# A hybrid decoder block on one core: softmax rows divided at the head's output, a scaling in eight steps, head products two tiles behind, and one Strassen product split in the led pairs

## The chip, the cores and the metric

The kernel runs as one program on 1 core of one Trainium2 chip. The metric is the time of one execution on the device in microseconds (us), the median of several runs. TensorE (PE) makes the matrix products and the transposes, VectorE (DVE), ScalarE (ACT) and GpSimd (POOL) the work on vectors, and SyncE (SP) issues the transfers, in the order of its queue.

## The reference

```python
hn = rmsnorm(h, norm_mix)
(fq, fk, fv, ff, gq, gk, gv, ga, gb, gz, gate_fox, gate_gdn) = split_in(hn @ w_in)
# forgetting attention, 8 heads of 128, causal, 1024 positions
s = fq @ fk.T * Dh ** -0.5 + (c[:, None] - c[None, :])      # c: cumulative log of the forget gate
y_fox = softmax(where(causal, s, -inf)) @ fv
# gated delta rule on conv + silu of gq, gk, gv, in chunks of 64
u = inverse(I + A) @ (beta * (v - decayed k @ state)); o = q @ state + attn @ u
y_gdn = rmsnorm(o, gdn_norm) * silu(gz)
y = sigmoid(gate_fox) * (y_fox @ w_branch_fox) + sigmoid(gate_gdn) * (y_gdn @ w_branch_gdn)
h = h + y @ w_out
up = causal_dwconv(rmsnorm(h, norm_ffn) @ w_up, ffn_conv_w)  # 3 taps, 2 x 2816 channels
u_gate, u_val = split(up, 2)
out = rmsnorm(h + (silu(u_gate) * u_val) @ w_down, norm_final)
```

Sequence and model width are 1024, one layer, one sequence, all in float32. (These lines are a condensed form of the reference; the delta rule is written as one step of its chunked form.)

## The kernel before

Every large product is made in float32 precision from two fp32r parts, high (`h`) and low (`l`), by three matmuls: high by high, low by high, high by low. `split` makes them: ACT casts the high part (L106), DVE or POOL subtracts it to get the low part (L107).

The stages follow one another: `head_in` (normalises x, transposes it, starts the small projections; 0 to 121 us), `project` (32 Strassen jobs of 84 matmuls, 121 to 821 us), the mix of attention and delta rule (to about 1094 us), the merge of the branches (to 1261), `mix_out` (to about 1390), `ffn_up` (to 1799) and `ffn_down`. The large products go through `strassen`, Winograd's form with seven half-size products a job of 12 matmuls each (P1 to P7 by the block that they take: `11`, `21`, `t2`, `t3`, `t1`, `22`, `t4`). The bank `a` gathers P1, then t2, t1 and 22 on top, and ACT copies it out between them as `x1`, `x2`, `x3` (L258), so the next product into `a` waits for the copy; DVE adds `c` (L289, L300, L315) from banks and copies. The first jobs of a stage can be *led*: `lead` holds products already made ahead, so that job has no P1 of its own between `t1` and `22`. This is so for the first pairs of `ffn_up`.

In `project` other work runs between the matmuls, paced by `left`, the matmuls still to do (from 2688 down): the convolutions of the heads, then `inverse`, a forward substitution of all 64x64 triangular blocks at once on DVE (`invz`, `invt`; L949 the scaling by beta, `invb`, then L961 and L963 a product and a subtraction for each of its pieces). `inverse` yields after each piece; `project` takes `INVERSE_STEPS` of them evenly between the start and the point where 480 matmuls are left.

In the mix, PE alternates between two streams. `fox` takes head after head: `probs` makes the scores of eight tiles t of 128 queries (softmax row by row: DVE adds the bias and finds the maximum, L1113, ACT makes the exponential and its sum, L1119, DVE the reciprocal, L1120, and the row is scaled, on ACT at L1122 for t under 5 or in head 0, else on POOL in two halves, L1125); `attend` transposes the rows (L1146), splits them, and makes the product with the values in halves of four tiles into the bank `ya` (L1137); ACT copies it out as `ye` (L1165), and SP writes it. The `scan` is the delta rule: per chunk the products into one of three banks `us` (L1260, L1265, L1271, L1272, L1274), with `su` (ACT, L1267), `sr` and `ss` (DVE), the output `o` (DVE, L1282) and its square sum `sjk` (ACT, L1284). `prep` loads a head's inputs for the scan (`skt`, `svt` and others) and POOL scales two of them (L1234).

The order on PE is that of the program. The order on DVE, ACT, POOL and SP is chosen when the kernel is built, by a scheduler with a cost model, except where `keep_in_program_order` holds an instruction to its place. Each queue runs strictly in order.

Of the kernel before, what the change touches and what calls it, by code (L numbers as in the profile page):

```python
# [17 lines left out]
P = 128  # L18
# [3 lines left out]
NT = S // P  # L22
# [53 lines left out]
def inverse_pieces(m):  # L76

    n = m + 1
    step = 512 // n
    return [(c0, min(c0 + step, Q)) for c0 in range(n, Q, step)]  # L80


INVERSE_STEPS = 10 + sum(len(inverse_pieces(m)) for m in range(Q))

EARLY = 3

# [1 line left out]
class Block:  # L88
# [88 lines left out]
    def strassen(self, jobs, blk, lead=(), pace=1, first=None, later=None, then=None):  # L177

        nc, sx = self.nc, self.sx
        v = nc.vector
        product, bank = self.block_product, self.bank
        n = len(jobs)

        def comb(x, y, op):  # L200
            t = sx.tile([P, 512], F32, tag="ws", bufs=4, name="ws")
            v.tensor_tensor(t, x, y, op)  # L202
            return t

        def weights(i):
            if first and i == 0:
                return None, None, None, first[0][:, 512:1024]
            w1, w2 = self.wload(jobs[i][0]), self.wload(jobs[i][1])
            return w1[:, 0:512], w1[:, 512:1024], w2[:, 0:512], w2[:, 512:1024]

        def summed(i):

            return lead[i][1] if i < len(lead) else None

        def operands():

            a = weights(0)
            if not lead:
                yield self.operand(a[0])
            for i in range(n):  # L220
                a11, a12, a21, a22 = a
                if not summed(i):
                    yield self.operand(a12)
                if first and i == 0:
                    yield from first[1]
                    s4 = None
                else:
                    s1 = comb(a21, a22, ALU.add)
                    s2 = comb(s1, a11, ALU.subtract)
                    yield self.operand(s2)  # L230
                    yield self.operand(comb(a11, a21, ALU.subtract))
                    yield self.operand(s1)
                    s4 = comb(a12, s2, ALU.subtract)
                if i + 1 < n:
                    a = weights(i + 1)
                    if i + 1 >= len(lead):
                        yield self.operand(a[0])
                if s4 is not None:
                    yield self.operand(s4)
                yield self.operand(a22)  # L240

        def lookahead(m):
            queue = []
            for o in operands():
                queue.append(o)
                if len(queue) > m:
                    yield queue.pop(0)
            for o in queue:
                if then:
                    next(then)  # L250
                yield o

        def temp(tag):
            return self.cx.tile([P, 512], F32, tag=tag, bufs=1, name=tag)

        def copied(tag, x):
            t = temp(tag)
            nc.scalar.copy(t, x)  # L258
            return t

        left, right = slice(0, 512), slice(512, 1024)
        ops = lookahead(3)
        rest = []

        def advance():
            m = pace
            while m and rest:
                if next(rest[0], DONE) is DONE:
                    rest.pop(0)
                else:  # L270
                    m -= 1

        def chunk(name):
            return self.cx.tile([P, S], F32, tag="c", bufs=self.nc_, name=name)

        if lead:
            a = lead[0][0]
        else:
            a = bank()
            yield from product(a, next(ops), blk["11"], True)  # L280
        p1 = None if summed(0) else copied("x1", a)
        for i, (_, _, done) in enumerate(jobs):
            c1 = chunk("c1")
            if summed(i):
                nc.scalar.copy(c1[:, left], summed(i))
            else:
                b = bank()
                yield from product(b, next(ops), blk["21"], True)
                v.tensor_tensor(c1[:, left], b, p1, ALU.add)  # L289
            advance()  # L290
            yield from product(a, next(ops), blk["t2"], False)
            u = copied("x2", a)
            advance()
            d = bank()
            yield from product(d, next(ops), blk["t3"], True)
            advance()
            yield from product(a, next(ops), blk["t1"], False)
            w = copied("x3", a)
            c2 = chunk("c2")
            v.tensor_tensor(c2[:, right], d, w, ALU.add)  # L300
            advance()
            if i + 1 < n:
                if i + 1 < len(lead):
                    a1 = lead[i + 1][0]
                else:
                    a1 = bank()
                    yield from product(a1, next(ops), blk["11"], True)
                p1 = None if summed(i + 1) else copied("x1", a1)
                advance()
            yield from product(a, next(ops), blk["22"], False)  # L310
            nc.scalar.copy(c1[:, right], a)
            rest.append(done(0, c1))
            advance()
            yield from product(d, next(ops), blk["t4"], False)
            v.tensor_tensor(c2[:, left], d, u, ALU.add)  # L315
            rest.append(done(1, c2))
            advance()
            if i + 1 < n:
                a = a1
        if later is not None:  # L320
            later.extend(rest)
        else:
            for r in rest:
                finish(r)
# [216 lines left out]
    def head_in(self, blk, right):  # L541
# [3 lines left out]
        with tc.tile_pool(name="hin", bufs=1) as pool, ExitStack() as px:  # L545
# [55 lines left out]
            for t in range(NT):  # L601
                xt = xp.tile([P, D], F32, tag="x", bufs=3, name="xt")
                nc.sync.dma_start(xt, a["x"][t * P:(t + 1) * P, :])
                if t == 0:
                    params = self.parameters()
                    take(params, 1)
                xn = self.norm_rows(xt, xp, "x")
                if t == 0:
                    w0 = wgroup(0, nc.vector)
                elif t == 2:  # L610
                    finish(params)
                columns(xn, t)
                if t:
                    rows(0, t - 1, *w0)
            rows(0, NT - 1, *w0)
            px.close()
            blk.update(self.blocks(right.enter_context(tc.tile_pool(name="hnt", bufs=1, side="right", reuse_waits="tile")),
                                   ("t1", "t2", "t3", "t4")))
# [92 lines left out]
    def project(self, blk, fox_pool):  # L711
# [159 lines left out]
        with ExitStack() as ix:  # L871
            for i, _ in enumerate(self.strassen(jobs, blk, pace=3)):
# [24 lines left out]
                    begin, steps = left, 0  # L897
                elif prep is None:

                    if (begin - left) * INVERSE_STEPS >= (begin - 480) * steps:  # L900
                        steps += 1
                        if not take(inv, 1):
                            ix.close()
# [17 lines left out]
    def inverse(self, ip):  # L921
# [21 lines left out]
            nc.sync.dma_start(br[s * Q:(s + 1) * Q, :], self.br_d[:, s * Q:(s + 1) * Q])  # L943
        for r in range(4):
            nc.sync.dma_start(z[:, 16 * r:16 * r + 16], self.z_d[:, 16 * r:16 * r + 16])
        for r in range(4):
            yield
            sl = slice(16 * r, 16 * r + 16)
            nc.vector.tensor_tensor(z[:, sl], z[:, sl], br.unsqueeze(1).to_broadcast([P, 16, Q]), ALU.mult)  # L949

        nc.vector.memset(z.rearrange("p m c -> p (m c)")[:, ::Q + 1], 1.0)
        yield
# [121 lines left out]
    def fox_first(self, pool):  # L1074

        self.fox_in = pool
        self.qh, self.ql, self.kh, self.kl = (pool.tile([P, S], F32R, name=n) for n in ("qh", "ql", "kh", "kl"))
        self.cr, self.cd = (pool.tile([P, S], F32, name=n) for n in ("cr", "cd"))
        self.vl = pool.tile([P, NT, P], F32R, name="vl")
# [13 lines left out]
    def probs(self, h, t, pts):  # L1093
# [2 lines left out]
        n = (t + 1) * P  # L1096
        tsl = slice(t * P, n)
        w = n if t < 4 else n // 2
        p = (pool if t < EARLY else self.probs_pool if t < 4 else self.probs_late).tile([P, n], F32, tag=f"p{t}", name=f"p{t}")
        mx = pool.tile([P, 4], F32, tag="mx", bufs=4, name="mx")  # L1100
        top = NEG
        for lo in range(0, n, w):
# [14 lines left out]
        mm = pool.tile([P, 2], F32, tag="mm", bufs=4, name="mm")  # L1117
        nc.vector.tensor_scalar(mm[:, 0:1], top, -1.0, None, op0=ALU.mult)
        nc.scalar.activation(p, p, AF.Exp, bias=mm[:, 0:1], accum_out=mm[:, 1:2])  # L1119
        nc.vector.reciprocal(mm[:, 1:2], mm[:, 1:2])  # L1120
        if t < 5 or h == 0:
            nc.scalar.activation(p, p, AF.Copy, scale=mm[:, 1:2])  # L1122
        else:
            for sl in (slice(0, w), slice(w, n)):
                nc.gpsimd.tensor_tensor(p[:, sl], p[:, sl], mm[:, 1:2].to_broadcast([P, w]), ALU.mult)  # L1125
        pts.append(p)

    def attend(self, h, half, pts):
        nc, pool, vh, vl, vf = self.nc, self.attend_pool, self.vh, self.vl, self.vf
        yps = self.acc.tile([P, 512], F32, tag="ya", bufs=1, name="ya")  # L1130
        last = 4 * half + 3
        queue = []

        def product():
            j, off, ops = queue.pop(0)
# [26 lines left out]
        yield  # L1162
        product()
        ye = pool.tile([P, 512], F32, tag="ye", bufs=1, name="ye")
        nc.scalar.copy(ye, yps)  # L1165
        nc.sync.dma_start(self.yf_d[h][:, half * 512:(half + 1) * 512], ye)

    def fox(self, pools, scan_pool):
# [28 lines left out]
    def mix(self, fp, pool, before_last):  # L1197
        tc, nc, a = self.tc, self.nc, self.a
        self.yf_d, self.yg_d = ([self.dr.tile([P, S], F32, name=f"{n}{h}") for h in range(H)] for n in ("yfd", "ygd"))
        if True:  # L1200
# [50 lines left out]
            def scan(h):  # L1251
# [4 lines left out]
                for n in range(NB):  # L1256
# [24 lines left out]
                        st = s2  # L1281
                    nc.vector.tensor_copy(o[:, n, :], op)  # L1282
                    jk = pool.tile([P, P], F32, tag="sjk", bufs=1, name="sjk")
                    nc.scalar.activation(jk, op, AF.Square, accum_out=sumo[:, n:n + 1])  # L1284
                    yield
                outs[h] = o, sumo

# [649 lines left out]
```

## Time and profile before

| what | value |
| --- | --- |
| median of 3 runs | 2024.65 us (2017.56, 2024.65, 2027.99) |
| profiled execution | 2024.17 us, span 2022.5 us |
| mean granted TensorE clock | 0.989 |
| busy: PE, DVE, ACT, POOL | 1924.2, 1476.1, 1075.7, 960.4 us |
| transfers | 350.96 MB, mean 174 GB/s |

An engine's busy time is a union over the whole span. A row of *waits* says which instruction of an engine waited for which one of another: total us, how often, the longest. A row of *lines* gives an instruction's line, engine, kind, output and inputs, shape, count, busy us and mean ns, and the idle time ahead of it with what ended it. A row of the *timeline* begins with the start and the duration in us, and for a group of instructions of one kind ("x4") it gives the stretch of the group. A row of *windows* gives the busy time of every engine in a stretch, then PE's granted clock (1.00 is full).

### The profile page before, as it was taken

The page shows a single profiled execution, that of the slowest core. Times are in us where ns is not written, and L with a number is a line of the kernel's source. Part 1 is how long each engine was busy: PE and PEld are TensorE (multiplying, and loading weights), DVE is VectorE, ACT ScalarE, POOL GpSimd, SP SyncE. Part 2 cuts the span into 40 slices and gives each one's busy share as a digit, 9 for nine tenths or more (in the row PEclk, how much of TensorE's full clock was granted, in tenths as well). Part 3 has the DMA queues.
Part 4 walks back from the last instruction along what each step waited for, and adds up shares of the span by engine and source line. Part 5 has one row for each costly group of instructions (what it writes and reads, how often), then busy time and mean ns, then how long its engine had stood idle before and what let it go on. Part 6 is the DMA issues. An engine that isn't in the chain of part 4 may idle for free. (4 is left out here: it accounts for less than half of the span.)

```text
span 2022.5 us, 29211 instructions
## 1 busy us (share of the span) xinstructions
PE 1924.2 (95%) x9628; PEld 1603.7 (79%) x9628; DVE 1476.1 (73%) x2546; ACT 1075.7 (53%) x2354; POOL 960.4 (47%) x818
## 2 busy tenths in 40 slices
PE   7999999998999999889998999999999999999998
PEld 6988887886777788778887787877788888877886
DVE  7848888866999864576777798667866767777535
ACT  5436777752334455565766444466655555553234
POOL 4735656554544545365675123145566566530012
PEclk9999999998999999998999999999999999999999
DMA  5235565565232494765754853664334343368654
GB/s 193 70 103 159 180 194 185 185 202 182 94 111 100 128 328 147 235 224 165 237 178 162 288 168 115 200 216 165 130 131 136 116 145 126 113 229 330 222 188 161
DMA packets 191848, 350.96 MB, mean 174 GB/s; under 512 B 50960, under 2 KB 79952, under 8 KB 191696
## 3 DMA queue, kind: packets, MB, share of 16 engines
q1 hardware_dynamic: 191552, 348.56, 51.3%
q8 instruction: 76, 1.25, 0.3%
q10 hardware_dynamic: 144, 0.52, 0.1%
q14 instruction: 76, 0.62, 0.1%
HBM read 232.79 MB, written 116.23 MB: 173 GB/s over the span
## 5 line engine op out<-in xcount | busy, mean ns | idle before, releaser
L107 POOL TENSOR_TENSOR ol<-ws,oh 128x512 fp32r<-128x512 f32 x212 | 285.6, 1350 | 254.0 <-ACT oh L106 248.7
L107 POOL TENSOR_TENSOR ol<-wr,oh 128x512 fp32r<-128x512 f32 x165 | 228.2, 1385 | 262.0 <-ACT oh L106 228.3
L106 ACT CAST oh<-ws 128x512 fp32r<-128x512 f32 x212 | 130.8, 618 | 185.2 <-PE mm L156 175.7
L202 DVE TENSOR_TENSOR ws<-wr 128x512 f32<-128x512 f32 x106 | 102.1, 963 | 138.8 <-DMA wr<-in_w_up_dram 82.6
L106 ACT CAST oh<-wr 128x512 fp32r<-128x512 f32 x204 | 123.4, 615 | 123.5 <-PE mm L156 85.4
L377 DVE SCALAR_TENSOR_TENSOR cv<-c,fw,cv 128x512 f32<-128x512 f32 (+2 forms) x176 | 127.4, 748 | 15.3 <-ACT cv L372 13.9
L377 DVE SCALAR_TENSOR_TENSOR cv<-c,cw,cv 128x511 f32<-128x511 f32 (+2 forms) x144 | 106.1, 749 | 7.9 <-ACT cv L372 6.0
L156 PE MATMUL mm<-bt4h,oh 128*128 128x512 f32 x216 | 86.9, 402 | 13.7 <-DVE c L300 13.7
L258 ACT COPY x<-mm 128x512 f32<-128x512 f32 x158 | 91.8, 581 | 4.5 <-PE mm L156 4.5
L156 PE MATMUL mm<-b22h,oh 128*128 128x512 f32 x216 | 86.1, 399 | 8.6 <-ACT x L258 8.4
L156 PE MATMUL mm<-bt1h,oh 128*128 128x512 f32 x216 | 85.2, 394 | 5.1 <-ACT x L258 4.9
L107 DVE TENSOR_TENSOR ol<-wd,oh 128x512 fp32r<-128x512 f32 x66 | 46.4, 705 | 58.9 <-ACT oh L106 58.9
L961 DVE TENSOR_TENSOR invt<-invz 128x399 f32<-128x399 f32 (+50 forms) x114 | 88.8, 792 | 0.4
L156 PE MATMUL mm<-bt4l,oh 128*128 128x512 f32 x216 | 87.4, 405 | 0.0
L156 PE MATMUL mm<-b22l,oh 128*128 128x512 f32 x216 | 86.1, 398 | 0.0
L156 PE MATMUL mm<-b21l,oh 128*128 128x512 f32 x216 | 86.0, 398 | 0.0
L156 PE MATMUL mm<-b11h,oh 128*128 128x512 f32 x216 | 85.0, 394 | 1.0 <-ACT oh L106 1.0
L156 PE MATMUL mm<-bt2h,oh 128*128 128x512 f32 x216 | 84.5, 391 | 1.5 <-ACT x L258 1.5
L156 PE MATMUL mm<-bt4h,ol 128*128 128x512 f32 x216 | 85.7, 397 | 0.0
L156 PE MATMUL mm<-bt2l,oh 128*128 128x512 f32 x216 | 85.2, 394 | 0.3 <-DVE bt2l L107 0.3
L156 PE MATMUL mm<-b11h,ol 128*128 128x512 f32 x216 | 84.9, 393 | 0.6 <-POOL ol L107 0.6
L156 PE MATMUL mm<-b11l,oh 128*128 128x512 f32 x216 | 85.2, 395 | 0.0
(406 smaller groups left out, 6377.7 us busy)
## 6 DMA issues: line engine op xcount, KB each, us to landing
wr<-in_w_up_dram SPq DMA_DIRECT2D x43, 512.0 KB, 3.9
wr<-in_w_gdn_dram SPq DMA_DIRECT2D x24, 512.0 KB, 3.8
wr<-in_w_out_dram SPq DMA_DIRECT2D x24, 512.0 KB, 3.7
s<-hy SPq DMA_DIRECT2D x44, 256.0 KB, 3.4
s<-z SPq DMA_DIRECT2D x44, 256.0 KB, 3.5
wd<-in_w_down_dram SPq DMA_DIRECT2D x44, 256.0 KB, 6.0
b22h<-s SPq DMA_DIRECT2D x44, 256.0 KB, 2.8
b22l<-s SPq DMA_DIRECT2D x44, 256.0 KB, 3.2
```

Of the source, the lines that this page charges most:

```text
L106: nc.scalar.copy(hi, src)
L107: (lo_eng or nc.vector).tensor_tensor(lo, src, hi.bitcast(F32), ALU.subtract)
L156: self.nc.tensor.matmul(ps, lhs[:, sl], rhs[:, k, :], start=(first and k == 0 and i == 0), stop=(k == 3 and i == 2), skip_group_check=True)
L202: v.tensor_tensor(t, x, y, op)
L258: nc.scalar.copy(t, x)
L377: nc.vector.scalar_tensor_tensor(t[:, lo:], c[:, 512 * j + lo - s:512 * (j + 1) - s], w[:, n - 1 - s:n - s], t[:, lo:], op0=ALU.mult, op1= ...
L961: nc.vector.tensor_tensor(tv, z[:, m:n, 0:n].to_broadcast([P, r, n]), z[:, m, c0:c1].unsqueeze(2).to_broadcast([P, r, n]), ALU.mult))
```

## The change

The change has five parts.

1. *Softmax at the head's output.* The rows p stay undivided. The reciprocals of four tiles are gathered in `rc` and written to DRAM (`rs_d`, 128x4 elements, after t = 3 and t = 7). `attend` reads them back as a row of 512 broadcast to all partitions (`rb`), and DVE multiplies the product `yps` by it into `ye` in place of ACT's copy.
2. *The inverse's scaling* is eight steps of 128x512 after five empty steps, held in program order; it was four of 128x1024. `INVERSE_STEPS` grows by nine, and the pace runs to 400 matmuls left.
3. *Head.* The small projections of a tile (`rows`) are made two tiles behind its transposes (`columns`).
4. *Led pairs.* In jobs whose next job is led, six of the twelve matmuls of `t3` (P7 in the change's words) stand before `t1` and six after it, so behind the copy x3.
5. *Scan.* The square sum reads `o` in SBUF, where it read the PSUM bank.

The diff, cut to its core:

```diff
-INVERSE_STEPS = 10 + sum(len(inverse_pieces(m)) for m in range(Q))
+INVERSE_STEPS = 19 + sum(len(inverse_pieces(m)) for m in range(Q))
...
-            yield from product(d, next(ops), blk["t3"], True)
+            p7 = product(d, next(ops), blk["t3"], True)
+
+            for _ in range(6 if i + 1 < len(lead) else 12):
+                next(p7)
+                yield
             advance()
             yield from product(a, next(ops), blk["t1"], False)
             w = copied("x3", a)
+            yield from p7
...
-                if t:
-                    rows(0, t - 1, *w0)
-            rows(0, NT - 1, *w0)
+                if t > 1:
+                    rows(0, t - 2, *w0)
+            for t in (NT - 2, NT - 1):
+                rows(0, t, *w0)
...
-                    if (begin - left) * INVERSE_STEPS >= (begin - 480) * steps:
+                    if (begin - left) * INVERSE_STEPS >= (begin - 400) * steps:
...
-        for r in range(4):
+        for _ in range(5):
             yield
-            sl = slice(16 * r, 16 * r + 16)
-            nc.vector.tensor_tensor(z[:, sl], z[:, sl], br.unsqueeze(1).to_broadcast([P, 16, Q]), ALU.mult)
+        for r in range(8):
+            yield
+            sl = slice(8 * r, 8 * r + 8)
+            tc.keep_in_program_order(nc.vector.tensor_tensor(z[:, sl], z[:, sl], br.unsqueeze(1).to_broadcast([P, 8, Q]), ALU.mult))
...
-        nc.vector.reciprocal(mm[:, 1:2], mm[:, 1:2])
-        if t < 5 or h == 0:
-            nc.scalar.activation(p, p, AF.Copy, scale=mm[:, 1:2])
-        else:
-            for sl in (slice(0, w), slice(w, n)):
-                nc.gpsimd.tensor_tensor(p[:, sl], p[:, sl], mm[:, 1:2].to_broadcast([P, w]), ALU.mult)
+        if t % 4 == 0:
+            self.rc = pool.tile([P, 4], F32, tag="rc", bufs=3, name="rc")
+        nc.vector.reciprocal(self.rc[:, t % 4:t % 4 + 1], mm[:, 1:2])
+        if t % 4 == 3:
+            nc.sync.dma_start(self.rs_d[h][t - 3:t + 1, :].rearrange("t q -> q t"), self.rc)
...
+        rb = pool.tile([P, 512], F32, tag="rb", bufs=2, name="rb")
+        nc.sync.dma_start(rb, self.rs_d[h][4 * half:4 * half + 4, :].rearrange("t q -> (t q)").partition_broadcast(P))
...
-        nc.scalar.copy(ye, yps)
+        nc.vector.tensor_tensor(ye, yps, rb, ALU.mult)
...
-                    nc.scalar.activation(jk, op, AF.Square, accum_out=sumo[:, n:n + 1])
+                    nc.scalar.activation(jk, o[:, n, :], AF.Square, accum_out=sumo[:, n:n + 1])
```

How the order moves is shown at three places. The first is DVE at the start of `inverse` in `project`; `ws` are sums of Strassen operands, `c` the sums of banks (L289, L300, L315 before; L289, L305, L320 after). Before:

```order
L949 TENSOR_TENSOR invz<-invz,invb 128x1024 x4
L202 TENSOR_TENSOR ws<-wr,ws 128x512
L951 MEMSET invz 128x64
L961 TENSOR_TENSOR invt<-invz 128x63
L963 TENSOR_TENSOR invz<-invz,invt 128x63
L961 TENSOR_TENSOR invt<-invz 128x124
L963 TENSOR_TENSOR invz<-invz,invt 128x62x2
L961 TENSOR_TENSOR invt<-invz 128x183
L963 TENSOR_TENSOR invz<-invz,invt 128x61x3
L961 TENSOR_TENSOR invt<-invz 128x240
L963 TENSOR_TENSOR invz<-invz,invt 128x60x4
L300 TENSOR_TENSOR c_5445<-mm,x_5443 128x512
```

After:

```order
L957 TENSOR_TENSOR invz<-invz,invb 128x512 x8
L202 TENSOR_TENSOR ws<-wr,ws 128x512
L959 MEMSET invz 128x64
L969 TENSOR_TENSOR invt<-invz 128x63
L971 TENSOR_TENSOR invz<-invz,invt 128x63
L969 TENSOR_TENSOR invt<-invz 128x124
L971 TENSOR_TENSOR invz<-invz,invt 128x62x2
L969 TENSOR_TENSOR invt<-invz 128x183
L971 TENSOR_TENSOR invz<-invz,invt 128x61x3
L969 TENSOR_TENSOR invt<-invz 128x240
L305 TENSOR_TENSOR c_5422<-mm,x_5420 128x512
L971 TENSOR_TENSOR invz<-invz,invt 128x60x4
```

The scalings stand ahead of the same `ws`, as one block of eight where there was one of four, and the `c` add behind the first inverse pieces stands one row earlier.

The second is POOL in the mix at the third head's rows, where `svt`, `vl` and `kl` are the scan's inputs, the low parts of the values and of the keys. Before:

```order
L1234 TENSOR_TENSOR svt<-svt,brk 128x512 x2
L1125 TENSOR_TENSOR p_9229<-p_9229,mm 128x384 x2
L1063 TENSOR_TENSOR vl<-vl,vh 128x512 x2
L1125 TENSOR_TENSOR p_9287<-p_9287,mm 128x448 x2
L1125 TENSOR_TENSOR p_9326<-p_9326,mm 128x512 x2
L107 TENSOR_TENSOR kl<-kl,kh 128x512 x2
```

After, at the same place:

```order
L1313 TENSOR_TENSOR so<-so,srs 128x512 x2
L1071 TENSOR_TENSOR vl<-vl,vh 128x512 x2
L1246 TENSOR_TENSOR skt<-skt,dkl 128x512 x2
L1246 TENSOR_TENSOR svt<-svt,brk 128x512 x2
L107 TENSOR_TENSOR kl<-kl,kh 128x512
```

The six scalings of p are gone from between the scan's inputs and the keys, and the casts of the values stand ahead of `skt`.

The third is SP in the mix at the loads for the sixth head, which `attend` of the fifth starts (`kl`, `ql`, `cr`: keys, queries and bias rows), with `ygd` and `yfd` the outputs of the scan and of the attention. Before:

```order
L1042 DMA kl<-kd_1559 128x1024
L1042 DMA ql<-qd_1551 128x1024
L1067 DMA cr<-rows 128x1024
L1314 DMA ygd_8318<-yge 128x512 x2
L1166 DMA yfd_8312<-ye 128x512
L1292 DMA sgz<-gzd_1565 128x1024
L1042 DMA vl<-vd 128x8x128
L1206 DMA sat<-a21d_1544 64x512
```

After:

```order
L1134 DMA rsd_7763<-rc 128x4x1
L1050 DMA kl<-kd_1559 128x1024
L1050 DMA ql<-qd_1551 128x1024
L1075 DMA cr<-rows 128x1024
L1144 DMA rb<-rsd_7763 128x512
L1326 DMA ygd_8328<-yge 128x512
L1134 DMA rsd_7763<-rc 128x4x1
L1326 DMA ygd_8328<-yge 128x512
L1304 DMA sgz<-gzd_1565 128x1024
L1144 DMA rb<-rsd_7763 128x512
L1178 DMA yfd_8322<-ye 128x512
L1050 DMA vl<-vd 128x8x128
```

The writes `rsd` and the loads `rb` are new; the first `rb` stands behind `kl`, `ql` and `cr` here, and the write of the second half behind a write `ygd`.

More of the change, by code (lines that the diff above doesn't have):

```diff
@@ L1076, in fox_first @@
         self.fox_in = pool
+        self.rs_d = [self.dr.tile([NT, P], F32, name=f"rsd{h}") for h in range(H)]
         self.qh, self.ql, self.kh, self.kl = (pool.tile([P, S], F32R, name=n) for n in ("qh", "ql", "kh", "kl"))
@@ L1098, in probs @@
         w = n if t < 4 else n // 2
-        p = (pool if t < EARLY else self.probs_pool if t < 4 else self.probs_late).tile([P, n], F32, tag=f"p{t}", name=f"p{t}")
+        home = pool if t < EARLY else self.probs_pool if t < 4 else self.probs_late
+        p = home.tile([P, n], F32, tag=f"p{t}", name=f"p{t}")
         mx = pool.tile([P, 4], F32, tag="mx", bufs=4, name="mx")
```

## The prediction

> **What bounds the kernel now.** I read the busy table of the page first, then the chain that ended last, then TensorE's idle time stage by stage (the waits of PE in a window), and where a wait is long, the timeline of the engine that releases it.
>
> ```profile
> PE 1924.2 (95%) x9628; PEld 1603.7 (79%) x9628; DVE 1476.1 (73%) x2546; ACT 1075.7 (53%) x2354; POOL 960.4 (47%) x818
> PE 31%; DVE 3%; ACT 1%; DMA 1%; issue 1%; POOL 1%; SPq 0%; POOLq 0%; ACTq 0%; DVEq 0%
> ```
>
> TensorE is the bound: busy for 1924.2 of 2022.5 us. No part of the change takes a matmul away, so all that can be won is the 98.3 us in which PE stands still and what is lost in the half-clock spells behind those stands. The question for each part is which of these stands it removes, and what is late next.
>
> **Head: rows two tiles behind.** PE's waits of the first 60 us (the first row) and of 13 to 60 us (the other three), then one row each of PE's and DVE's timeline:
>
> ```profile
> PE ms L588 <- DVE nxn L538: 9.8, 2, 7.7
> PE ms L572 <- DVE b12l L107: 1.4, 3, 0.7
> PE ms L572 <- DVE b11l L107: 1.2, 2, 0.6
> PE ms L572 <- DVE b22l L107: 1.0, 2, 0.6
> 13.41 0.57 PE L570 MATMUL ms<-vwh,b11h 128*128 128x262 f32 x1
> 13.59 0.76 DVE L538 TENSOR_SCALAR nxn<-xt,nrs 128x1024 f32<-128x1024 f32 x1 [0.65 <-POOL nrs L395]
> ```
>
> The 9.8 us for the first two normalised tiles stay. The other 3.6 us are matmuls that wait for a split which DVE makes only after the tile's transposes; a second tile of distance covers them. Against it: tile 2's transposes now come before the first rows at 13.41, and its nxn is ready only at 13.59 + 0.76 = 14.35. That is a new wait of about 0.9 us. Gain 3.6 - 0.9 = 2.7 at best; with DVE's work unchanged in front of it some of the splits stay late, so I take **-1.5** (range -3 to +2, the latter if the start at half clock is prolonged by the new wait).
>
> **Inverse: eight paced steps.** PE's waits of 486 to 700 us, DVE's timeline, its inverse group by line, and windows (us, PE, PEld, DVE, ACT, POOL busy, granted clock, DMA share, GB/s):
>
> ```profile
> PE mm L156 <- DVE c L300: 12.7, 3, 7.3
> PE mm L156 <- ACT x L258: 3.8, 4, 1.5
> 485.25 7.46 DVE L949 TENSOR_TENSOR invz<-invz,invb 128x1024 f32<-128x1024 f32 x4 [5.93 <-DMA invb<-brd]
> 496.23 0.68 DVE L300 TENSOR_TENSOR c<-mm,x 128x512 f32<-128x512 f32 x1
> L961 DVE TENSOR_TENSOR invt<-invz 128x399 f32<-128x399 f32 (+50 forms) x114 | 88.8, 792 | 0.4
> 490.00:500.00 10.00, 3.03 (x7) 2.46 (x8) 9.58 (x19) 0.61 (x2) 1.42 (x1) 0.59 0.37 107
> 500.00:520.00 20.00, 19.99 (x84) 16.08 (x84) 19.83 (x34) 6.29 (x11) 8.73 (x7) 0.95 0.23 79
> 562.00:568.00 6.00, 5.23 (x16) 4.16 (x17) 6.00 (x13) 0.62 (x1) 0.59 (x2) 0.72 0.43 160
> ```
>
> DVE sits 5.93 us before the invb rows land, then makes 7.46 us of scaling and eleven short inverse instructions, and only then the c add (L300) that frees PE's bank: 7.3 us of wait. The words of the change suggest that this one goes. The order says otherwise: the eight 128x512 scalings stand in one block, at the place where the four 128x1024 stood, and the add comes behind one row less (L963 of 0.40 us leaves its front). The scaling itself is the same number of elements; four more starts cost at most 4 x 0.1 us, bounded by the 0.11 us of the shortest DVE row there is around it (the memset). So the first wait stays: about 0, between -4 (if the five empty steps ahead let invb land before DVE reaches the block) and +1.
>
> What does move is everything behind. Before, 124 steps are paced to end when 480 matmuls are left, now 133 when 400 are; a step still comes every 8.2 matmuls, but five steps are empty and four more go to the scaling, so at a given c add nine fewer inverse pieces stand ahead. At 0.79 us for the first instruction of a piece alone that is 7.1 us; by the order with the durations of the trace it is 8 to 10 us less work of DVE ahead of each L300 after the third. DVE is full there (19.83 of 20 us), so these c adds were late by queueing. The later waits are 12.7 - 7.3 = 5.4 us for c and 3.8 for x, and the half-clock spell behind the 562 us wait costs (1 - 0.72) x 6.0 = 1.7: together 10.9 us. The pieces taken from the front come back at the end, over 80 more matmuls, so the same work is spread only 7% thinner and some waits will stay. I take **-8.5** of the 10.9 (range -13 to 0).
>
> **Mix: the softmax division at the head's output.** PE's waits of 820 to 1113 us; groups by line; the timelines of ACT, POOL and PE at the fourth head (h = 3); three windows:
>
> ```profile
> PE ms L1146 <- POOL p L1125: 7.7, 4, 3.2
> PE us L1260 <- ACT sjk L1284: 4.4, 3, 2.1
> PE us L1271 <- ACT su L1267: 4.3, 6, 1.5
> PE ya L1137 <- POOL vl L1063: 2.9, 4, 1.6
> PE us L1265 <- POOL svt L1234: 1.1, 1, 1.1
> L1122 ACT ACTIVATE p<-p,mm 128x128 f32<-128x128 f32 (+7 forms) x43 | 27.2, 639 | 4.5 <-DVE mm L1120 2.9 <-DVE mm L1118 1.3
> L1125 POOL TENSOR_TENSOR p<-p,mm 128x384 f32<-128x384 f32 (+2 forms) x42 | 42.0, 1025 | 15.0 <-DVE mm L1118 7.9 <-DVE mm L1120 7.0
> L1165 ACT COPY ye<-ya 128x512 f32<-128x512 f32 x16 | 9.4, 587 | 9.5 <-PE ya L1137 8.8 <-PE ms L1108 0.7
> L107 DVE TENSOR_TENSOR pl<-ms,ph 128x512 fp32r<-128x512 f32 x48 | 32.3, 686 | 19.5 <-ACT ph L106 19.1
> 938.62 1.18 ACT L1119 ACTIVATE p<-p,mm 128x1024 f32<-128x1024 f32 x1
> 943.16 4.79 POOL L1125 TENSOR_TENSOR p<-p,mm 128x448 f32<-128x448 f32 x4
> 947.01 1.33 PE L1146 MATMUL ms<-ident,p 128*128 128x128 f32 x5 [2.54 <-POOL p L1125]
> 820.00:1113.00 293.00, 259.25 (x1813) 232.26 (x1812) 208.18 (x732) 190.86 (x528) 170.90 (x184) 0.96 0.62 206
> 944.00:952.00 8.00, 5.32 (x25) 5.13 (x26) 3.55 (x7) 1.73 (x4) 7.47 (x7) 0.61 0.12 45
> 982.00:990.00 8.00, 4.76 (x38) 4.49 (x38) 4.47 (x10) 2.98 (x9) 7.79 (x8) 1.00 0.40 133
> ```
>
> Removed: 27.2 us of ACT, 42.0 of POOL, and from ACT the 9.4 of ye; DVE gets 16 multiplications of 128x512 with PSUM, 16 x 0.686 = 11.0 us on 208. The fourth head shows the value: the exponential of p7 ended at 939.8, POOL finished scaling it only at 947, and PE's transposes waited for that. Without L1125 they wait for the exponential alone. So 7.7 us go, and with them (1 - 0.61) x 8 = 3.1 us of half clock here. The sjk wait (4.4) goes in part, since Square now reads o in SBUF and the bank is freed by DVE; su and vl (4.3 and 2.9) shrink, as their engines have shorter queues. In sum 7.7 + 3.1 + half of 11.6 = 16.6. Against it: DVE's 11.0 us, of which I charge a quarter, 2.8, since DVE is busy 71% of this stage; POOL's first preparation now stands skt, skt, vl, vl, svt, svt, so the 1.1 us wait for svt grows by up to two vl casts, about 2. That leaves 11.8, from which I take 1.8 off for what DVE's ye may still wait: **-10** (range -19 to +20, the upper end from that chain).
>
> *The new chain.* The sum's reciprocal of tile 3 is written out, read back as a 128x512 broadcast, and only then can DVE make ye of the first half. DVE's, ACT's and SP's rows at the fourth head, and issue-to-landing of a broadcast and of two loads of 4-byte elements:
>
> ```profile
> 931.17 0.16 DVE L1120 RECIPROCAL mm<-mm 128x1 f32<-128x1 f32 x1
> 943.82 0.59 ACT L1165 COPY ye<-ya 128x512 f32<-128x512 f32 x1
> 936.73 0.37 SPq L1067 DMA_DIRECT2D cr<-rows  x1
> cr<-rows SPq DMA_DIRECT2D x7, 512.0 KB, 6.7
> gn<-in_gdn_norm_dram SPq DMA_DIRECT2D x1, 0.5 KB, 1.9
> nf<-in_norm_ffn_dram SPq DMA_DIRECT2D x1, 4.0 KB, 6.3
> ```
>
> There are 943.8 - 931.3 = 12.5 us. The write (512 elements) lies between gn's 1.9 and nf's 6.3 (128 and 1024 elements), the broadcast at most cr's 6.7 (it is half as large): 8.6 to 13.0 us. That fits, by -0.5 to +4 us. For the second half there are about 21 us, from tile 7's reciprocal at 940.2 to ye at 961.7. I count the chain as hidden. The Trainium skill, "DMA: Bandwidth & Descriptors", rules for kernel authors, says that a strided last dimension lowers to one descriptor per element and should be rearranged; this speaks against the write. By it the write is 512 descriptors and stands nearer to nf than to gn, so the cover is all but gone; no run so far shows such a write.
>
> **Led pairs.** PE's waits of 1390 to 1447 us, and that window:
>
> ```profile
> PE mm L156 <- ACT x L258: 5.7, 4, 1.7
> PE mm L156 <- DVE c L300: 1.0, 2, 0.7
> 1390.00:1447.00 57.00, 50.34 (x215) 39.62 (x214) 44.97 (x60) 33.71 (x58) 29.64 (x23) 1.00 0.41 137
> ```
>
> Four waits of 1.4 us, each for the ACT copy of x3 that frees the bank before the next product. With six matmuls of P7, 6 x 0.23 = 1.4 us at the spacing that full clock gives here (84 matmuls in 20 us in the inverse's window is 0.24), standing behind P(t1), the copy is covered. DVE is busy 45 of 57 us and the c add now comes six matmuls earlier against the end of P7, so part returns as a wait for DVE: **-3** of 5.7 (range -5 to 0).
>
> **Sum**, against the profiled execution of 2024.17 us (1.67 around its span; the median of the three runs, 2024.65, stands 0.5 above it): -1.5 - 8.5 - 10 - 3 = -23, so 2001.2, on the median **2001.5 us**. Differences under 0.5%, 10 us, can't be told from none.
>
> **Rivals.**
> 1. *The scan eats the mix gain*: PE is released from p and waits at the next link, su, ss and o on ACT and DVE, as PE's six su waits suggest; against it, those engines are 65 to 71% busy. Mix gives 0: 2024.5 - 13 = 2011.5.
> 2. *The inverse does not change*: the block stands where it stood and DVE is full anyway, so the later waits only shift. Then 2001.5 + 8.5 = 2010.
> 3. *The other side: DVE stands at ye for rb.* For h = 4 and 5 the order has rb behind kl, ql and cr; cr was issued at 936.73, so rb lands at 937.1 + up to 6.7 = 943.8, with no margin, and SP, which waits in line for the write to land, sends the next loads later too. While DVE stands there, sr, pl and the scores stand behind it. It decides when the write and the broadcast take more than 12.5 us. Late by 5 us in eight first halves is 40 us; with 13 won elsewhere and 10 in the rest of the mix, 2024.5 + 17 = 2041; late by 2 us gives 2017.5. The rule on strided dimensions quoted above makes this rival likelier, and no row of the trace decides it.
> 4. *The clock gate hides gain*: the 2.54 us wait was followed by half clock (0.61 over 944 to 952), the 3.24 us one at 982 to 985 was not (1.00), so which spell goes is not set by length alone. If no spell goes, 3.1 + 1.7 us fewer are won: 2006. The Trainium skill, "TensorE: Matmul & The Clock Gate", Part 1, has the clock fall after an idle window of some 3.4 us that runs freely; by it no wait under that length would cost clock, and the 944 window disagrees, unless waits and thin work in one window add up.
>
> **How the numbers follow.** Forecast 0.48 (faster); rival 1 0.20 (just over the bound: 0.13 faster, 0.07 same); rival 2 0.12 (0.10, 0.02); rival 3 0.15 (0.07 same, 0.08 slower); rival 4 0.05 (faster). Faster 0.76, same 0.16, slower 0.08. The range goes from 1986 (mix and inverse near their best ends, -38) to 2020 (rival 3 late by 2 us); outside it I leave the larger half of rival 3 and a little at the low end. The likeliest case's own range is 1988 to 2010.
>
> **What would show it.** Right: no PE wait for p, fewer than 3 us for x L258 from 1390 to 1447, the 7 us wait at 490 still there and under 4 us of others behind it up to 700, ye on DVE with no wait for rb. Wrong: rows of DVE ye waiting for DMA rb; PE waits for sr, ss or su grown by 5 us or more; new waits on x or c where six matmuls of P7 now stand. The forecast fails most easily in the mix, whose range is the widest.

## The result, and the profile after

The changed kernel takes 2078.22 us (median of 4 runs, 2072.72 to 2082.63), the kernel before 2023.93 (4 runs): a ratio of 1.027, 95% interval 1.0233 to 1.0307. It is 54 us slower, where 23 us faster was forecast. The profiled execution took 2079.06 us with a span of 2077.3. Its busy row, beside the one shown before:

```profile
PE 1940.9 (93%) x9628; PEld 1619.7 (78%) x9628; DVE 1500.6 (72%) x2566; ACT 1048.5 (50%) x2295; POOL 931.5 (45%) x776
```

ACT and POOL did lose their work (27 and 29 us net), and PE still stands still for 38 us more; its busy time grew by 17 us too, at a lower granted clock: over the stretch of the transposes shown next it was 0.95 before and 0.88 after. Since PE's order is nearly the same in both, the start of the same instruction in both traces tells where. The transposes of the probabilities, from the first to the last, before and after (count, duration in ns, first and last start):

```profile
L1146 PE MATMUL ms<-ident,p x288: 270/273/473, 829.5 to 1088.6; 128*128 128x128 f32 x144
```

```profile
L1158 PE MATMUL ms<-ident,p x288: 270/273/422, 829.4 to 1146.3; 128*128 128x128 f32 x144
```

They begin at the same time and take 316.9 us where they took 259.1. The mix alone lost 57.8 us; all other stages together gained 3. Its waits of PE from 810 to 1170 us, DVE's two longest new ones and SP's longest (total us, times, longest):

```profile
PE ya L1149 <- DVE ye L1177: 19.5, 4, 8.5
PE ya L1149 <- ACT pf L1166: 12.6, 2, 7.4
PE us L1283 <- ACT su L1279: 7.5, 4, 5.2
PE ya L1149 <- ACT ph L106: 6.7, 2, 4.7
PE ms L1251 <- DMA sx<-xd: 5.6, 2, 3.4
...
DVE ye L1177 <- DMA rb<-rsd: 25.0, 6, 10.5
DVE ye L1177 <- DMA yfd<-ye: 6.8, 3, 5.3
...
SPq L1144 <- DMA rsd<-rc: 100.5, 12, 12.4
```

No wait for p is left. Instead DVE stands at ye for the broadcast row, SP stands 100 us in its queue for the written reciprocals to land, and PE waits for whatever stands behind either. The last head shows one turn of it in full (SP, DVE and PE):

```profile
1120.10 0.37 SPq L1134 DMA_DIRECT2D rsd<-rc  x1
1128.36 0.32 SPq L1144 DMA_DIRECT2D rb<-rsd  x1
1128.78 0.38 SPq L1134 DMA_DIRECT2D rsd<-rc  x1
1139.71 0.32 SPq L1178 DMA_DIRECT2D yfd<-ye  x1
1140.12 0.38 SPq L1144 DMA_DIRECT2D rb<-rsd  x1
...
1128.30 0.16 DVE L1132 RECIPROCAL rc<-mm 128x1 f32<-128x1 f32 x1 [0.52 <-ACT p L1129]
1138.99 0.69 DVE L1177 TENSOR_TENSOR ye<-ya,rb 128x512 f32<-128x512 f32 x1 [10.53 <-DMA rb<-rsd]
...
1139.83 0.77 PE L1149 MATMUL ya<-ph,vh 128*128 128x512 f32 x1 [8.45 <-DVE ye L1177]
```

The write of the first half was issued at 1120.10, and SP stood until it had landed, at 1128.36, before it could send the load of rb. DVE had nothing ahead of ye for the 10.53 us until rb landed, and PE stood 8.45 of them, since the one bank `ya` is free only when ye has read it. This rb went out 0.42 us ahead of the second half's write, and it landed late too: the trace has no packet of any transfer from 1134 to 1139 us, and still ye could begin only at 1138.99. The landings say what was slow (KB of each, median us from issue), before and after:

```profile
kl<-kd SPq DMA_DIRECT2D x7, 512.0 KB, 4.9
cr<-rows SPq DMA_DIRECT2D x7, 512.0 KB, 6.7
sxt<-yd SPq DMA_DIRECT2D x16, 128.0 KB, 4.4
```

```profile
rsd<-rc SPq DMA_DIRECT2D x16, 2.0 KB, 11.8
rb<-rsd SPq DMA_DIRECT2D x16, 256.0 KB, 5.3
kl<-kd SPq DMA_DIRECT2D x7, 512.0 KB, 9.4
cr<-rows SPq DMA_DIRECT2D x7, 512.0 KB, 10.5
sxt<-yd SPq DMA_DIRECT2D x16, 128.0 KB, 11.8
```

After the change the trace gives the landing of only few of them: one of the 16 writes, four of rb, three, two and six of kl, cr and sxt. SP's rows give more. In the twelve places where it waits for a write, 8.3 to 14.4 us pass from the issue of the write to that of rb (median 12.5), so the 11.8 stands for the rest. The loads near the writes land 4 to 7 us later than before.

### The profile page after: what moved, and what is told of

It reads as the page before. It is cut to its first block, busy times and chain, and to the rows that moved or that the text cites. A ratio compares the mean times of both kernels' runs of the same rounds, so it can differ in the third digit from the quotient of the medians.

```text
span 2077.3 us, 29178 instructions
## 1 busy us (share of the span) xinstructions
PE 1940.9 (93%) x9628; PEld 1619.7 (78%) x9628; DVE 1500.6 (72%) x2566; ACT 1048.5 (50%) x2295; POOL 931.5 (45%) x776
## 5 line engine op out<-in xcount | busy, mean ns | idle before, releaser
L202 DVE TENSOR_TENSOR ws<-wr 128x512 f32<-128x512 f32 x106 | 106.3, 1003 | 125.9 <-DMA wr<-in_w_up_dram 67.4
L156 PE MATMUL mm<-bt1l,oh 128*128 128x512 f32 x216 | 85.0, 394 | 0.0
```

Of the source, the lines that this page charges most:

```text
L156: self.nc.tensor.matmul(ps, lhs[:, sl], rhs[:, k, :], start=(first and k == 0 and i == 0), stop=(k == 3 and i == 2), skip_group_check=True)
```

## The experiments

Every time below is a median, with the ratio to the runs of the kernel before on the same chip (2026 to 2028 us in those groups).

**Which part: all but the softmax, and the softmax alone.** The first undoes part 1 in the changed kernel, the second makes part 1 alone in the kernel before; their diffs are the first part of the diff shown, backwards and forwards.

> The changed kernel with its first part undone: probabilities are scaled and ye is copied as before; inverse, head, led pairs and the scan's square stay changed. Theory W (the loss is the waiting for the written reciprocals): the mix is as before, and the stage differences of the changed kernel's trace remain, +1.8 head, +2.8 in project ahead of the inverse, -5.3 inverse, -3.6 led pairs: about 2020 us. Rival O (a part other than the softmax slows the mix, for instance the square of o read from SBUF): above 2050 us.

> The kernel before with the first part alone. Theory W: the mix loses the same 57 us, so about 2081 us, and DVE waits at ye for rb for some 25 us. Rival O: within 20 us of 2024.

Measured: 2020.84 us without it (ratio 0.9975, interval 0.9957 to 0.9993), as expected, and 2099.55 us with it alone (1.0369, 1.031 to 1.0428), 18 more than expected. The four other parts are worth about 5 us of gain, and the division at the head's output makes the whole loss. Alone it is worse than in company: its mix ran 337.3 us from the first to the last transpose. In that kernel the square still reads the bank, and PE waited 15.8 us for it, a wait that is not in the list of the changed kernel.

**Writing the reciprocals as rows.** The 128x4 tile is transposed on PE, and four runs of 512 bytes are written in place of 512 elements of 4 bytes.

```diff
...
+    def write_sums(self, h, half):
...
+        ps = self.small()
+        nc.tensor.transpose(ps[0:4, 0:P], self.rcs.pop(0), self.ident)
+        rr = self.attend_pool.tile([4, P], F32, tag="rr", bufs=2, name="rr")
+        nc.vector.tensor_copy(rr, ps[0:4, 0:P])
+        nc.sync.dma_start(self.rs_d[h][4 * half:4 * half + 4, :], rr)
...
```

> The changed kernel with the reciprocals of four tiles transposed on PE (128x4 to 4x128, 16 transposes), copied to SBUF by DVE and written as four rows of 512 bytes; the broadcast load stays. Theory W with the 4-byte elements as the cause of the late landing (11.8 us median): the write lands in under 4 us, SP and DVE hardly wait, the mix falls to or below the 265 us of before: 2005 to 2022 us. Rival C (the round trip through DRAM in SP's queue is too long however it is written): the landing stays near 8 us or more or the waits remain, above 2050 us.

Measured: 2021.86 us (0.9983, 0.9962 to 1.0004). The 54 us are gone, though the round trip through DRAM and the multiplication on DVE are still there: rb was waited for just once, for 0.3 us. A new wait took part of the gain, PE's own transposes of the reciprocals, which wait for them:

```profile
PE ms L1143 <- DVE rc L1133: 16.6, 9, 3.1
```

**Waiting or writing: rb from a constant row.** The row is in DRAM from the start of the attention; the writes of the reciprocals stay, and nobody reads them.

```diff
+        self.rs_c = self.dr.tile([4, P], F32, name="rsc")
+        self.nc.sync.dma_start(self.rs_c, self.ident[0:4, :])
...
-        nc.sync.dma_start(rb, self.rs_d[h][4 * half:4 * half + 4, :].rearrange(...).partition_broadcast(P))
+        nc.sync.dma_start(rb, self.rs_c.rearrange("t q -> (t q)").partition_broadcast(P))
```

> The changed kernel, but rb is read from a constant row that was written once at the start of the attention (so ye is multiplied by a wrong row), while the 16 writes of reciprocals stay and nobody waits for them. Theory W with waiting as the cost: no wait for rb, 2005 to 2025 us. Rival T (the 8192 elements of 4 bytes crowd the queues and slow the other loads, kl from 4.9 to 9.4 us and sxt from 4.4 to 11.8): the loads stay slow and the time stays above 2045 us.

Measured: 2068.47 us (1.0209, 1.0168 to 1.0249). This was the experiment that mattered. With the dependence gone only some 10 of the 54 us went; theory W had 2005 to 2025, and the time is rival T's, above 2045. The chain that I took for the whole cause from the changed kernel's waits was the smaller part.

**The same without the writes.**

> As the kernel whose rb is a constant row, but the 16 writes of reciprocals are left out too (the output is not the reference's). Theory E (the 4-byte elements of the write hold up every transfer in the queues behind it): the 48 us that the constant row alone still lost are gone, 2005 to 2020 us, landings of kl and cr back at 5 to 7 us. Rival M (the work moved to DVE and the changed order of the loads cost the time): 2050 us or more, no better than with the writes.

Measured: 2014.69 us (0.9936, 0.9912 to 0.9959). Sixteen writes of 2 KB that nobody waits for by data cost 2068.47 - 2014.69 = 53.8 us. Transposes from first to last, with the writes and without:

```profile
L1160 PE MATMUL ms<-ident,p x288: 270/273/473, 827.5 to 1134.0; 128*128 128x128 f32 x144
```

```profile
L1158 PE MATMUL ms<-ident,p x288: 270/273/421, 825.9 to 1074.7; 128*128 128x128 f32 x144
```

306.5 us against 248.8, and the latter is 10.3 less than the kernel before.

**What is dear about the write.** Four kernels keep the constant row and the unread writes of the same 2 KB, and change how these lie in DRAM: 128 runs of 16 bytes, or 512 elements of 4 bytes that lie 16, 64 or 512 bytes apart. By their traces every engine and SP run the same instructions in the same order in these four and in the kernel with the writes side by side, so that the five differ only in where the bytes go. (Without the write the order of the other instructions is not quite the same.)

```diff
-self.rs_d = [self.dr.tile([NT, P], F32, ...)]
+self.rs_d = [self.dr.tile([2, P, 4], F32, ...)]                  # runs of 16 bytes
+self.rs_d = [self.dr.tile([NT, P, 4], F32, ...)]                 # 16 bytes apart; 16 for 64, 128 for 512
-nc.sync.dma_start(self.rs_d[h][t - 3:t + 1, :].rearrange("t q -> q t"), self.rc)
+nc.sync.dma_start(self.rs_d[h][t // 4], self.rc)                 # runs of 16 bytes
+nc.sync.dma_start(self.rs_d[h][t - 3:t + 1, :, 0:1].rearrange("t q one -> q t one"), self.rc.unsqueeze(2))
```

> The constant row again, but the reciprocals are written in a layout of their own, 128 runs of 16 bytes in place of 512 elements of 4 bytes: the same bytes, a quarter of the elements, nobody reads them. Theory E with a price for each element: a quarter of the loss of the writes, about 2024 us (2010 plus 58 / 4). Rival B (any transfer far under 512 bytes an element costs the same, or the price is one for each transfer): 2055 us or more.

> The constant row and the 16 writes of 512 elements of 4 bytes, but each element goes to an address of its own, 512 bytes from the next; nobody reads them (the output is not the reference's). Theory N (the price is that of neighbouring 4-byte elements, which are written one after the other to the same stretch of memory): the loss of the writes goes, 2008 to 2020 us, and the loads behind land in 5 to 8 us. Rival S (the price is that of elements of 4 bytes as such, wherever they go): 2060 us or more, as with the elements side by side.

> The same with 64 bytes from one element to the next. Theory N with a stretch of 64 bytes: 2008 to 2020 us. Theory N with a stretch of 512 bytes: eight elements still share one, so a loss between the two, 2015 to 2060. Rival S: 2060 us or more.

> The constant row and the 16 unread writes of 512 elements of 4 bytes, now 16 bytes from one element to the next, so that four elements share 64 bytes where sixteen shared them side by side and none does at 64 bytes. If sharing as such costs (every element waits for its neighbour), a clear part of the 54 us stays: 2030 to 2060. If the price grows with how many share a stretch, about a quarter at most: 2010 to 2025. If it is only elements that touch each other: 2003 to 2012.

| the 2 KB as | time, us | ratio (95% interval) | third write, us | transposes, first to last |
| --- | --- | --- | --- | --- |
| 512 elements side by side | 2068.47 | 1.0209 (1.0168 to 1.0249) | 10.4, in the changed kernel | 306.5 |
| 512 elements, 16 bytes apart | 2015.17 | 0.9929 (0.9909 to 0.9948) | 3.5 | 249.6 |
| 512 elements, 64 bytes apart | 2006.82 | 0.9905 (0.9875 to 0.9935) | 2.3 | 245.9 |
| 512 elements, 512 bytes apart | 2008.45 | 0.9905 (0.9883 to 0.9927) | 1.8 | 244.4 |
| 128 runs of 16 bytes | 2008.20 | 0.9913 (0.9886 to 0.9941) | 1.9 | 242.7 |
| no write | 2014.69 | 0.9936 (0.9912 to 0.9959) | none | 248.8 |

The third write (second head, first half) moves its packets when nothing else does, so its landing is its own. In the changed kernel it is told by SP, which waits for it and goes on 10.4 us after the issue. The medians over all writes of a kernel, 5.6, 5.0, 5.0 and 4.9 us in the four new ones, mix such writes with those that stand behind loads.

The number of elements and their size are not the price: 512 elements of 4 bytes cost nothing that can be measured when they lie 64 bytes apart, as theory N had it. My expectation for the runs of 16 bytes, a quarter of the loss, was a miss; their loss is nil. What costs is how the elements lie: sixteen to each 64 bytes, each written by itself from another partition. Four to each 64 bytes do not show this loss, neither the elements 16 bytes apart nor the runs of 16 bytes, which lie side by side and come from neighbouring partitions too. At 16 bytes apart the time is 8 us above that at 64, but the two intervals overlap, so a small price is not shown in the time; the third write takes 3.5 us against 2.3. (2015 us lies in the range expected of a price that grows with how many share a stretch.) That writes to one stretch must follow each other is a likely reading; no trace shows what happens inside the memory.

How the unread write costs the others is seen in the 12 us from the issue of the fourth write on, in which both kernels issue the same nine transfers. First the elements side by side (884 to 896 us), then 64 bytes apart (874.7 to 886.7): the packets and bytes of the stretch, and the landing of the load that stands right behind the write.

```profile
DMA packets 2216, 2.11 MB, mean 176 GB/s; under 512 B 1674, under 2 KB 1674, under 8 KB 2214
skt<-ktd SPq DMA_DIRECT2D x1, 512.0 KB, 12.2
```

```profile
DMA packets 2852, 4.08 MB, mean 340 GB/s; under 512 B 1742, under 2 KB 1742, under 8 KB 2850
skt<-ktd SPq DMA_DIRECT2D x1, 512.0 KB, 6.2
```

In both the DMA engines read as busy nearly throughout, and beside the elements that lie side by side they move half as much. PE then waits at the next links of the chain. Over the transposes it stands still for 57 us with the elements side by side and for 19 with them 64 bytes apart, and its granted clock is 0.88 against 0.97.

**Towards a faster kernel.** The transposes of the reciprocals are moved one tile later for the first half, and to the end of the first half for the second; then fourteen empty steps stand ahead of the inverse's scaling; then the head is put back.

```diff
-        if t == 5:
+        if t == 6:
             self.write_sums(h, 0)
...
-                    if half == 0 and i == 1:
+                    if half == 0 and i == 4:
                         self.write_sums(h, 1)
```

> The row write, with its transposes of the sums one tile later for the first half and at the end of the first half for the second, so that PE does not meet the reciprocals before they are ready. Theory: the 16.6 us in which PE waited for a reciprocal there mostly go: 2006 to 2014 us. Rival: the broadcast then lands too late and DVE waits at ye, or PE waits at the next link for the same exponentials: 2018 to 2030 us.

Measured: 2015.52 us (0.9936, 0.9917 to 0.9955), a little above the expected 2014. PE no longer waits for a reciprocal; DVE waited once, 2.0 us, for rb.

> The same with fourteen empty steps ahead of the inverse's scaling in place of five (the pace grows by nine steps): the c add behind the block then stands behind six scalings, where it stood behind eight and seven inverse instructions. Theory (the first wait of 7.2 us is DVE's queue in front of that add): it falls to 2 to 4 us, so 3 to 5 us less than the kernel with five empty steps. Rival: the pieces come back later as waits for c, no difference of more than 2 us.

Measured: 2006.39 us (0.9894, 0.9872 to 0.9916), 9 us less than with five where 3 to 5 were expected. PE's waits of 486 to 700 us, with five empty steps and with fourteen:

```profile
PE mm L156 <- DVE c L305: 7.2, 1, 7.2
PE mm L156 <- ACT x L258: 5.4, 5, 1.7
```

```profile
PE mm L156 <- ACT x L258: 3.5, 3, 1.7
PE mm L156 <- DVE c L305: 3.4, 1, 3.4
```

The first wait halves and nothing takes its place. That accounts for 5.7 us; the rest of the 9 is not traced.

> The row write with the later transposes and fourteen empty steps, and the head as it was before the change (rows one tile behind). If two tiles behind cost 1 to 2 us, as the traces show (PE's waits for nxn of 14 to 16 us where there were 9.8, against 3.6 us of waits for splits that went), this comes out 1 to 2 us below the 2006.4 us of that kernel, which is within what the timing can tell; if two tiles behind gain 1.5 us as forecast, it comes out above.

Measured: 2005.68 us (0.9889, 0.9868 to 0.9911), no different from 2006.39. This last version is the fastest tried, 1.1% under the kernel before and 3.5% under the changed one (2005.68 / 2078.22). PE's waits of its first 60 us for the normalised tiles, with rows one tile behind and two:

```profile
PE ms L593 <- DVE nxn L543: 10.2, 2, 7.5
```

```profile
PE ms L593 <- DVE nxn L543: 14.3, 5, 7.6
```

## Why the prediction was wrong

**The step that failed** is the one that sized the new chain: "The write (512 elements) lies between gn's 1.9 and nf's 6.3". It took 8.3 to 14.4 us where SP waited for it, about twice the upper bound in the median (12.5). The two rows were loads of 4-byte elements from DRAM; they said nothing of a write of neighbours into DRAM, and I had no row of one. By those bounds the chain fitted into its 12.5 us, so I counted it as hidden; with 11.8 + 5.3 = 17.1 us it could not be. This accounts for the smaller part of the miss. The larger part is a term that the sum does not have: it prices the write by who waits for it, and what the write does to the transfers beside it stands in it at nothing.

The mix's term was -10 and came out at +57.8. The experiments split the difference of 68 us. Taking the writes away gives 248.8 us between the transposes where there were 259.1: the removed scalings, the smaller queues of ACT and POOL, and DVE's eleven us of ye together are worth -10.3. In the four kernels with a cheap write it is -9.5 to -16.4. The forecast of -10 lies in that span; how much each of its terms gave, the runs do not separate. The writes, unread, add 57.7 (306.5 - 248.8), and the waiting for them by data 10.4 more (316.9 - 306.5).

**Rival 3** named the side, the place and one of the mechanisms: DVE at ye for rb, and SP in line for the write. It had 0.15. But its price was only the waiting, and that is 2078.22 - 2068.47, some 10 us. What it lacked is that the write holds up the transfers beside it: it had SP send the next loads later, and in the kernel with the unread writes, where SP does not stand in line for rb, they are sent and land late all the same. The Trainium skill's page "DMA: Bandwidth & Descriptors", quoted for its rule on strided last dimensions, was the page to read: by it an element is a descriptor, and the trace agrees: one such write made 528 packets, 16 more than its elements. They are all in the stretch from 868.3 to 870 us, in which nothing else moved:

```profile
DMA packets 528, 0.00 MB, mean 1 GB/s; under 512 B 528, under 2 KB 528, under 8 KB 528
```

SP had issued the write at 868.05 and went on, when it landed, at 878.42:

```profile
868.05 0.37 SPq L1134 DMA_DIRECT2D rsd<-rc  x1
878.42 0.32 SPq L1144 DMA_DIRECT2D rb<-rsd  x1
```

So the packets had gone within two us of the issue, and the landing came eight later. The same write with its elements 64 bytes apart has the same 528 packets, and there it has landed 2.3 us after the issue. The Trainium skill says on the same page, under its specifications, that transfers under 512 bytes make the engine read, modify and write. By that the runs of 16 bytes and the elements 64 bytes apart would pay too. They cost nothing here, so for this kernel the measurement goes against taking the size for the price.

**The inverse**, forecast -8.5: the stretch from the start of the inverse's transposes to the first scores went from 345.5 to 340.2 us, -5.3. The reading of the order was right: the block stayed, and the first wait with it. Of the rest, all waits for c went, as forecast:

```profile
PE mm L156 <- DVE c L305: 7.2, 1, 7.2
PE mm L156 <- ACT x L258: 5.0, 5, 1.7
```

The waits for x did not go, they rose from 3.8 to 5.0. They are ACT's copies, which I had taken to be late for the same reason as DVE's adds. The half-clock spell went with the c waits (the granted clock is 1.00 from 560 to 590 us). These two (5.4 + 1.7) less the rise of 1.2 are 5.9, near the 5.3 that were won.

**Led pairs**, forecast -3: the waits of these jobs fell from 5.7 for x and 1.0 for c to the first row below, -3.8; the second stood in the kernel before too, ahead of the window shown.

```profile
PE mm L156 <- ACT x L258: 2.9, 4, 1.6
PE mm L156 <- DVE bt2l L107: 0.3, 1, 0.3
```

**Head**, forecast -1.5: the waits for splits went, 3.6 us, but the transposes now wait for nxn three times more, 15.7 us in all where there were 9.8. The 0.9 us that I charged was for one tile, and three tiles paid. The project began at 123.7 us in this trace and 121.9 before; over eleven profiles with two tiles behind it began at 121.6 to 123.7, over the three with one at 121.9 to 122.7. The term is nil.

**Project ahead of the inverse**, forecast at nothing, lost 2.8 us (328.7 to 331.5 from its first matmul to the inverse's transposes); ACT's squares are waited for 3.6 us where it was 0.8. No experiment was made on it.

No experiment was made on the clock (rival 4). It had its part in the loss: over the stretch of the transposes PE was busy for 233.8 us before at a granted clock of 0.95, and for 251.3 after at 0.88, with nearly the same number of matmuls.

## What to carry to other kernels

Bound an operation that the trace does not have by rows of the same direction and layout, or give it no bound: two small loads said nothing about a scattered write. When a small transfer lands late, ask not only who waits for it but what stands behind it in the queues: take the wait away and leave the transfer, then take the transfer away, and the two prices come apart. Where a per-partition column has to become a row in DRAM, transposing it on PE and writing whole rows costs 16 short transposes here and saves more than 50 us.

## What the runs showed of the hardware

Sixteen writes of 512 4-byte elements each, side by side in DRAM and read by nobody, cost 60 to 62 us, 3.8 us each, against the same writes with the elements 512 or 64 bytes apart in kernels of the same order (53.8 against the kernel without them). The stage moves 206 GB/s in the kernel before. One such write, alone in the queues, had landed 10.4 us after its issue, although its packets had left in under two; with the elements 64 bytes apart the same write takes 2.3 us and the cost is gone. Loads beside such a write land late: 12.2 us for one where it is 6.2. (The kernels with the elements 64 or 512 bytes apart, or in runs of 16 bytes, are even 6 to 8 us under the one with no write; its loads stand in another order, and I did not follow that up.) A wide gap in the trace between a write's last packet and its landing is the sign to look for.
